# Conditioning loads in their own ring, a first stage on three engines, and a pre-repeated condition vector

## The chip, the cores and the metric

One core of one Trainium2 chip runs the kernel. The metric is the device time of one execution in microseconds (us), lower is better. The kernel before took 1848.71 us (median of 3 runs, 1846.3 to 1849.69).

## The reference

Two decoder layers over 512 tokens with 1024 channels, all in float32. Each layer modulates its input by scale and shift vectors computed from a condition vector `c`, runs a token mixer with three branches, normalises, modulates again and runs a convolutional feed-forward network. Cut to what the change touches:

```python
cond = jax.nn.silu(c)                                   # (1, 1024)
for l in range(2):
    mod = cond @ w_ada[l] + b_ada[l]                    # 6 vectors of 1024
    sh1, sc1, g1, sh2, sc2, g2 = split(mod, 6)
    h = x * (1.0 + sc1) + sh1
    y = _token_mixer(h, ...)                            # retention, HGRN2, convolution, gates, w_out
    x = _layer_norm(ALPHA * x + g1 * y, ln1_g[l], ln1_b[l])
    h = x * (1.0 + sc2) + sh2
    y = _conv_ffn(h, ...)
    x = _layer_norm(ALPHA * x + g2 * y, ln2_g[l], ln2_b[l])
```

## The kernel before

Channels lie on the 128 partitions and tokens along the free axis, so a 1024-channel tensor is 8 tiles of 128 x 512. To keep float32 accuracy every large product is made of three matmuls on rounded parts: an operand is split into a high part `hi` (ScalarE copy to a rounded type) and a rest `lo` (VectorE subtract), and `mm3` adds hi x hi, hi x lo and lo x hi in PSUM (lines 249 to 251).

**Weights** come in chunks of 128 x 1024 (512 KB), in one fixed order per layer. `prefetch` (line 203) takes a tile `wr` of the ring with the tag `raw` (4 buffers), issues its load on SyncE's queue (L215), and writes `wh` (ScalarE, L216) and `wl` (VectorE, L217) into rings of 4. One chunk feeds 24 matmuls. `chunk` calls `prefetch` so that two chunks beyond the one in use have been asked for.

**Conditioning columns.** `ada_col(l, i)` (line 189) makes one column of 128 modulation values: it takes a tile `ar` of the same ring `raw`, loads 512 KB of `w_ada` (L191), multiplies it with `cond` and sums along the row in one VectorE instruction (L195), and adds the bias into `modt` (L196). There are 48 columns for each layer. It is a generator in two steps: the load, then the arithmetic. `cond` is a 128 x 1024 tile that holds silu(c) in every partition.

**The first stage** (lines 692 to 706) does this for j = 0 to 7: two columns of layer 0 (shift and scale of channel tile j), the load of `X[j]`, one weight chunk, and then `hi` (ScalarE, L702), a full-precision copy `f` (GpSimd, L703), `lo = f - hi` (VectorE, L704) and `X[j] *= ALPHA` (GpSimd, L705). Beside it `proj_octo` (line 265) runs 8 passes of 24 matmuls, pass j on the chunk and the `hi`, `lo` of tile j.

**Background work.** `fill` is a list of generators that `tick` advances between groups of 12 matmuls: convolution taps, then `conv_norm` (which makes the branch output `u_c`), then `rest(aux)`, the 24 columns 16 to 39 of the layer. `heads` are the retention and HGRN2 heads. Columns 40 to 47, and the first 16 of layer 1, are put in `fill` during the feed-forward network.

**The branch loop** (lines 760 to 788) takes the branches in the order 1, 0, 2. For each of 4 column pairs jp it runs two gate projections (sigmoid on ScalarE, L767, which frees the PSUM tile) and the branch projection; VectorE multiplies the two (L782), GpSimd adds the product to `ys[j]` (L786), and in the third branch `split` makes `hi` and `lo` of `ys[j]` (L229, L231). The output projection (line 794) then reads all 8 `ys`.

**Order.** The framework lays out each engine's instructions ahead of time, in a fixed order that follows a model of when operands are ready, with the order of the program as priority. On the chip each engine then works through its list in that order. A tile waits until the buffer of its ring that it takes is released.

Of the kernel before, what the change touches and what calls it, by code (L numbers as in the profile page):

```python
# [10 lines left out]
F32 = mybir.dt.float32  # L11
# [3 lines left out]
AF = mybir.ActivationFunctionType  # L15
ALU = mybir.AluOpType
# [4 lines left out]
P = 128  # L21
# [5 lines left out]
FT = DFF // P  # L27
ALPHA = (2.0 * L) ** 0.25
EPS = 1e-5
NB = 47  # L30
NHL = 4
LA = 2
NRAW = 4
TK = 1.7
AUX = 99
TG = 1.1
# [53 lines left out]
def trunk(ctx, tc, xT, cT, pos, ada, bada, wts, cols, lbl, rope_c, decay, hmask, outT):  # L90
    nc = tc.nc
    mm = nc.tensor.matmul
    act = nc.scalar.activation
# [4 lines left out]
    pts = nc.gpsimd.tensor_scalar  # L98

    const = ctx.enter_context(tc.tile_pool(name="const", bufs=1))  # L100
    wp = ctx.enter_context(tc.tile_pool(name="wp", bufs=1))
# [5 lines left out]
    def nm(s):  # L107
        n_[0] += 1
        return f"{s}{n_[0]}"

    def big(dt=F32, w=S):
        return bp.tile([P, w], dt, tag="B", name=nm("b"), bufs=NB)

    def hbuf():
        return bp.tile([P, S], F32R, tag="H", name=nm("h"), bufs=16)
# [4 lines left out]
    def pm():  # L120
        return pp.tile([P, S], F32, tag="pm", name=nm("pm"), bufs=4)
# [8 lines left out]
    def const_tile(shape, name, dt=F32):  # L130
        return const.tile(shape, dt, tag=name, name=name)
# [7 lines left out]
    nc.vector.tensor_copy(avg_r, avg_x)  # L139

    cond = const_tile([P, D], "cond")
    nc.sync.dma_start(cond, cT.partition_broadcast(P))
    act(cond, cond, AF.Silu)
    bad = const_tile([P, 48 * L], "bad")
    nc.sync.dma_start(bad, bada)
# [11 lines left out]
    def mod(l, s, j):  # L157
        return modt[l][:, s * 8 + j:s * 8 + j + 1]
# [28 lines left out]


    def ada_col(l, i):
        raw = wp.tile([P, 1024], F32, tag="raw", name=nm("ar"), bufs=NRAW)  # L190
        nc.sync.dma_start(raw, ada[l, i])  # L191
        o = ADA[i]
        dst = modt[l][:, o:o + 1]
        yield 0.0
        stt(raw, raw, 1.0, cond, ALU.mult, ALU.mult, accum_out=dst)  # L195
        ts(dst, dst, bad[:, 48 * l + o:48 * l + o + 1], 1.0 if o // 8 in (1, 4) else 0.0, ALU.add, ALU.add)  # L196
        yield 1.3
# [5 lines left out]
    def prefetch(n=1):  # L203
        for _ in range(n):
            if wnext[0] == L * NW:
                return
            l, i = divmod(wnext[0], NW)
            wnext[0] += 1
            raw = wp.tile([P, 1024], F32, tag="raw", name=nm("wr"), bufs=NRAW)
            hi = wp.tile([P, 1024], F32R, tag="hi", name=nm("wh"), bufs=NHL)  # L210
            lo = wp.tile([P, 1024], F32R, tag="lo", name=nm("wl"), bufs=NHL)
            n = 512 if l == 0 and i == 0 else 1024
            for o in range(0, 1024, n):
                s = slice(o, o + n)
                nc.sync.dma_start(raw[:, s], wts[l, i][:, s])  # L215
                act(hi[:, s], raw[:, s], AF.Copy)  # L216
                tt(lo[:, s], raw[:, s], hi.bitcast(F32)[:, s], ALU.subtract)  # L217
            ready.append((W_PLAN[l][i][0], (hi, lo)))

    def chunk(kind, ahead=LA):  # L220
        prefetch(ahead + 1 - len(ready))
        k, w = ready.pop(0)
        assert k == kind, (k, kind)
        return w
# [30 lines left out]

    def proj(w, xs, us=TK):
        q = pm()
        n = len(xs)
        for k in range(n):
            mm3(q, sl2(w, 128 * k), xs[k], k == 0, k == n - 1)  # L260
            if k % 4 == 3:
                tick(us)
        return q
# [292 lines left out]
    X = [const_tile([P, S], f"x{j}") for j in range(8)]  # L556
# [136 lines left out]
    for j in range(8):  # L693
        cs = [ada_col(0, 2 * j), ada_col(0, 2 * j + 1)]
        for g in cs:
            next(g)
        nc.sync.dma_start(X[j], xT[j])
        for g in cs:
            next(g)
        prefetch()  # L700
        hi, lo, f = hbuf(), hbuf(), big()
        act(hi, X[j], AF.Identity, bias=mod(0, 0, j), scale=mod(0, 1, j))  # L702
        pts(f, X[j], mod(0, 1, j), mod(0, 0, j), ALU.mult, ALU.add)  # L703
        tt(lo, f, hi.bitcast(F32), ALU.subtract)  # L704
        pts(X[j], X[j], ALPHA, None, ALU.mult)  # L705
        hs.append((hi, lo))

    for l in range(L):
# [3 lines left out]
        acc, u_a, u_b, u_c = [], [None] * NH, [None] * NH, []  # L712
        CS = [big(), big()]
        aux = [ada_col(l, i) for i in range(16, 40)]
        if l == 0:
            tables()
# [43 lines left out]
        for bi, b in enumerate(ORDER):  # L760
            us = (u_a, u_b, u_c)[b]
            for jp in range(4):
                sg = []
                for t in range(2):
                    q = proj(chunk("in"), hs, TG if bi == 2 else TK)
                    s = big()
# [9 lines left out]
                for t in range(2):  # L776
                    j = 2 * jp + t
# [39 lines left out]
        for _ in first:  # L817
            pass

        fill.extend(ada_col(l, i) for i in range(40, 48))  # L820
        gs = []

# [161 lines left out]
```

## Time and profile before

| | before |
|---|---|
| median of 3 runs | 1848.71 us |
| profiled execution, device time | 1850.63 us |
| span of the profile | 1848.5 us |
| granted clock over the span | 0.995 |
| TensorE (PE) busy | 1805.8 us |
| VectorE (DVE) busy | 1292.6 us |
| ScalarE (ACT) busy | 748.4 us |
| GpSimd (POOL) busy | 225.8 us |

The profiled execution took 1850.63 us, 2.1 us more than its span, and 1.9 us more than the median of the runs. All durations below are from this execution. Ends of matmuls are modelled and overlap, so that the spacing of matmul starts, and not their durations, tells the pace.

### The profile page before, as it was taken

The numbers are of one execution on the slowest core, as the hardware profiler recorded it, in microseconds if no ns is written. First come the engines' busy times: TensorE is split into PE (matmuls) and PEld (weight loads), VectorE is DVE, ScalarE is ACT, GpSimd is POOL, SyncE is SP. The second block draws the span as 40 slices with busy tenths as digits, with TensorE's granted clock in tenths as the row PEclk, the third lists the DMA queues.
The fourth block names the chain that finished last, engine by engine and source line by source line (L and its number), as shares of the span: only waits on it lengthen the run. The fifth ranks groups of instructions, "written<-read, shape, count | busy, mean of one in ns | idle before, by whom it ended". The sixth has DMA issues, their size and how long they took to land.

```text
span 1848.5 us, 23499 instructions
## 1 busy us (share of the span) xinstructions
PE 1805.8 (98%) x9156; PEld 1520.1 (82%) x9156; DVE 1292.6 (70%) x2026; ACT 748.4 (40%) x1034; POOL 225.8 (12%) x193
## 2 busy tenths in 40 slices
PE   7999999999999999999999999999999999999997
PEld 5888877888788888888889987778788988888886
DVE  6995565977869756667499565993775896666354
ACT  2434344333337444422263344453523464444222
POOL 3111231042100000000000221320322000000002
PEclk9999999999989999999999999999999999999998
DMA  8512222226614422255222121222474243222221
GB/s 301 197 69 80 75 75 80 91 104 212 230 70 142 144 102 92 102 182 184 93 87 103 69 75 69 80 74 99 161 241 148 92 146 128 103 92 102 92 80 46
DMA packets 63614, 217.81 MB, mean 118 GB/s; under 512 B 7440, under 2 KB 9872, under 8 KB 63504
## 3 DMA queue, kind: packets, MB, share of 16 engines
q1 hardware_dynamic: 63504, 216.32, 34.0%
q8 instruction: 72, 1.18, 0.3%
q14 instruction: 38, 0.31, 0.0%
HBM read 214.19 MB, written 2.10 MB: 117 GB/s over the span
## 4 chain that ended last, share of the span: by engine, by line
PE 81%; DVE 10%; DMA 3%; issue 2%; POOL 2%; ACT 2%; POOLq 0%; SPq 0%; DVEq 0%; ACTq 0%
PE pm L249 24%; PE pm L251 24%; PE pm L250 24%; DMA ar<-ada 3%; DVE wl L217 2%; PE ps L477 2%; POOL b L786 1%; DVE ar L195 1%; DVE b L383 1%; DVE x L642 1%; PE po L552 1%; PE ps L544 1%; DVE b L782 1%; PE ps L250 1%; PE ps L251 0%
## 5 line engine op out<-in xcount | busy, mean ns | idle before, releaser
L249 PE MATMUL pm<-h,wh 128*128 128x512 f32 (+1 forms) x1568 | 612.7, 391 | 13.7 <-ACT wh L216 12.1
L251 PE MATMUL pm<-h,wl 128*128 128x512 f32 (+1 forms) x1568 | 602.6, 384 | 0.1
L250 PE MATMUL pm<-h,wh 128*128 128x512 f32 (+1 forms) x1568 | 601.6, 384 | 0.0
L217 DVE TENSOR_TENSOR wl<-wr,wh 128x1024 fp32r<-128x1024 f32 (+1 forms) x301 | 376.4, 1253 | 250.5 <-ACT wh L216 249.4
L216 ACT ACTIVATE wh<-wr 128x1024 fp32r<-128x1024 f32 (+1 forms) x301 | 317.1, 1055 | 489.3 <-PE pm L250 387.2
L249 PEld LDWEIGHTS pm<-h,wh 128*128 128x128 f32 x1568 | 295.5, 188 | 72.9 <-ACT wh L216 12.1
L251 PEld LDWEIGHTS pm<-h,wl 128*128 128x128 f32 x1568 | 295.0, 188 | 61.1 <-DVE wl L217 3.1
L250 PEld LDWEIGHTS pm<-h,wh 128*128 128x128 f32 x1568 | 295.4, 188 | 58.7 <-issue 1.9
L249 PE MATMUL pm<-b,wh 128*128 128x512 f32 (+1 forms) x764 | 280.6, 367 | 5.6 <-ACT b L229 4.2
L250 PE MATMUL pm<-b,wh 128*128 128x512 f32 (+1 forms) x764 | 279.6, 366 | 0.3 <-DVE b L231 0.2
L251 PE MATMUL pm<-b,wl 128*128 128x512 f32 (+1 forms) x764 | 279.0, 365 | 0.0
L383 DVE SCALAR_TENSOR_TENSOR b<-b,cols,b 128x511 f32<-128x511 f32 (+14 forms) x240 | 171.6, 769 | 0.0
L249 PEld LDWEIGHTS pm<-b,wh 128*128 128x128 f32 x764 | 144.8, 190 | 30.3 <-ACT b L229 5.4
L250 PEld LDWEIGHTS pm<-b,wh 128*128 128x128 f32 x764 | 144.9, 190 | 24.5 <-DVE b L231 1.5
L251 PEld LDWEIGHTS pm<-b,wl 128*128 128x128 f32 x764 | 145.0, 190 | 22.8
L195 DVE SCALAR_TENSOR_TENSOR ar<-ar,cond 128x1024 f32<-128x1024 f32 x96 | 123.8, 1296 | 57.1 <-DMA ar<-ada 56.9
L229 ACT ACTIVATE b<-b 128x512 fp32r<-128x512 f32 x88 | 55.5, 630 | 232.8 <-DVE b L832 109.2
L231 DVE TENSOR_TENSOR b<-b,b 128x512 fp32r<-128x512 f32 x88 | 61.1, 694 | 53.8 <-ACT b L229 53.6
L490 POOL TENSOR_TENSOR b<-b,b 128x256 f32<-128x256 f32 x64 | 56.4, 881 | 324.1 <-PE ps L477 217.3
L786 POOL TENSOR_TENSOR b<-b,b 128x512 f32<-128x512 f32 x32 | 57.2, 1786 | 234.9 <-DVE b L782 222.5
L249 PE MATMUL pm<-wh,h 128*128 128x256 f32 x256 | 73.6, 288 | 0.0
L250 PE MATMUL pm<-wl,h 128*128 128x256 f32 x256 | 72.3, 283 | 0.6 <-DVE wl L217 0.6
(205 smaller groups left out, 1904.1 us busy)
## 6 DMA issues: line engine op xcount, KB each, us to landing
wr<-wts SPq DMA_DIRECT2D x299, 512.0 KB, 3.5
ar<-ada SPq DMA_DIRECT2D x96, 512.0 KB, 4.3
x<-xT SPq DMA_DIRECT2D x8, 256.0 KB, 5.9
b<-decay SPq DMA_DIRECT2D x8, 256.0 KB, 3.7
outT<-b SPq DMA_DIRECT2D x16, 128.0 KB, 1.8
b<-hmask SPq DMA_DIRECT2D x3, 256.0 KB, 5.9
cond<-cT SPq DMA_DIRECT2D x1, 512.0 KB, 4.5
wr<-wts SPq DMA_DIRECT2D x2, 256.0 KB, 7.3
```

Source lines behind the costliest of these rows:

```text
L195: stt(raw, raw, 1.0, cond, ALU.mult, ALU.mult, accum_out=dst)
L216: act(hi[:, s], raw[:, s], AF.Copy)
L217: tt(lo[:, s], raw[:, s], hi.bitcast(F32)[:, s], ALU.subtract)
L229: act(hi, src, AF.Copy)
L231: tt(lo, src, hi.bitcast(F32), ALU.subtract)
L249: mm(dst, a[0], b[0], start=first, stop=False)
L250: mm(dst, a[0], b[1], start=False, stop=False)
L251: last[0] = mm(dst, a[1], b[0], start=False, stop=end)
L383: stt(a[:, d:S], us[i][:, 0:S - d], col(l, "cw", 4 * (CK - 1 - d) + i0 + i), a[:, d:S], ALU.mult, ALU.add)
L477: mm(z[:, 64 * i:64 * (i + 1)], ke[:, sl], rhs, start=True, stop=True)
L490: ptt(kv[:, :, 0, :], kv[:, :, 0, :], fv[:, :, 1:2].broadcast_to([P, nb, m]), ALU.mult)
L786: ptt(ys[j], ys[j], sg[t], ALU.add)
```

## The change

- `cT`, the input that `cond` is loaded from, becomes a 128 x 1024 array with the same row repeated by the host; the load reads 128 rows in place of one row 128 times.
- `ada_col` takes its tile from a ring of its own, tag `ada`, 3 buffers. `raw` keeps 4 buffers, now for weights alone.
- In the first stage GpSimd's two instructions go to ScalarE: `f` becomes a second `act` like `hi`, `X[j] *= ALPHA` an `act` with AF.Copy.
- The ring `B` of 128 x 512 tiles has 48 buffers in place of 47.
- The scratch area for software-made DMA descriptors is 1024 bytes; with it there is space for the new buffers.

```diff
-NB = 47
+NB = 48
+NADA = 3
@@
     cond = const_tile([P, D], "cond")
-    nc.sync.dma_start(cond, cT.partition_broadcast(P))
+    nc.sync.dma_start(cond, cT)
@@ def ada_col(l, i):
-        raw = wp.tile([P, 1024], F32, tag="raw", name=nm("ar"), bufs=NRAW)
+        raw = wp.tile([P, 1024], F32, tag="ada", name=nm("ar"), bufs=NADA)
@@
         act(hi, X[j], AF.Identity, bias=mod(0, 0, j), scale=mod(0, 1, j))
-        pts(f, X[j], mod(0, 1, j), mod(0, 0, j), ALU.mult, ALU.add)
+        act(f, X[j], AF.Identity, bias=mod(0, 0, j), scale=mod(0, 1, j))
         tt(lo, f, hi.bitcast(F32), ALU.subtract)
-        pts(X[j], X[j], ALPHA, None, ALU.mult)
+        act(X[j], X[j], AF.Copy, scale=ALPHA)
@@
-        "cT": np.ascontiguousarray(a["c"][0]),
+        "cT": np.repeat(a["c"], 128, axis=0),
@@
-    nc = _bacc.Bacc("TRN2", target_bir_lowering=False, num_devices=1)
+    nc = _bacc.Bacc("TRN2", target_bir_lowering=False, num_devices=1, dynamic_dma_scratch_size=1024)
```

## Rows read from the trace of the kernel before

**Rows 1.** The page, part 1: busy time of each engine, share, instructions.
```profile
PE 1805.8 (98%) x9156; PEld 1520.1 (82%) x9156; DVE 1292.6 (70%) x2026; ACT 748.4 (40%) x1034; POOL 225.8 (12%) x193
```

**Rows 2.** Timeline of the start: start, duration, engine, line, operation [idle before <-releaser].
```profile
4.82 4.55 SPq L191 DMA_DIRECT2D ar<-ada  x2
...
7.78 1.23 DVE L195 SCALAR_TENSOR_TENSOR ar<-ar,cond 128x1024 f32<-128x1024 f32 x1 [6.58 <-DMA ar<-ada]
...
9.41 0.43 SPq L697 DMA_DIRECT2D x<-xT  x1
...
12.07 0.79 PE L249 MATMUL pm<-h,wh 128*128 128x512 f32 x1 [12.07 <-ACT wh L216]
```

**Rows 3.** The page, part 6: DMA issues, count, KB each, median us to landing.
```profile
wr<-wts SPq DMA_DIRECT2D x299, 512.0 KB, 3.5
...
cond<-cT SPq DMA_DIRECT2D x1, 512.0 KB, 4.5
```

**Rows 4.** Timeline of PE: second pass of the first stage begins; next projection begins.
```profile
19.81 0.39 PE L249 MATMUL pm<-h,wh 128*128 128x512 f32 x1
...
59.53 0.40 PE L249 MATMUL pm<-wh,h 128*128 128x256 f32 x2
60.55 0.39 PE L250 MATMUL pm<-wl,h 128*128 128x256 f32 x1 [0.62 <-DVE wl L217]
```

**Rows 5.** Window: busy us (instructions) of each engine, granted clock, DMA share, GB/s.
```profile
1500.00:1550.00 50.00, 50.00 (x222) 41.44 (x221) 41.35 (x62) 23.95 (x32) 0.00 (x0) 1.00 0.49 166
```

**Rows 6.** Groups by line, 12 to 53 us: count, busy us, mean ns, idle before.
```profile
L702 ACT ACTIVATE h<-x,mod 128x512 fp32r<-128x512 f32 x7 | 5.7, 817 | 28.3 <-DVE mod L196 28.3
...
L704 DVE TENSOR_TENSOR h<-b,h 128x512 fp32r<-128x512 f32 x8 | 5.5, 693 | 7.6 <-POOL b L703 7.6
```

**Rows 7.** Timeline of PE, layer 0: last branch projection, output projection, marker L582.
```profile
494.19 0.39 PE L249 MATMUL pm<-b,wh 128*128 128x512 f32 x1
...
501.16 0.50 PE L249 MATMUL pm<-b,wh 128*128 128x512 f32 x1 [1.34 <-ACT b L767]
507.46 0.56 PE L249 MATMUL pm<-b,wh 128*128 128x512 f32 x1 [1.94 <-ACT b L229]
...
511.70 0.80 PE L249 MATMUL pm<-b,wh 128*128 128x512 f32 x1 [2.29 <-ACT b L229]
...
526.48 0.40 PE L582 MATMUL ps<-b,avg_r 128*128 128x512 f32 x1
```

**Rows 8.** Timeline of PE, layer 1: the same two ends.
```profile
1413.33 0.39 PE L249 MATMUL pm<-b,wh 128*128 128x512 f32 x1
...
1435.55 0.40 PE L582 MATMUL ps<-b,avg_r 128*128 128x512 f32 x1
```

**Rows 9.** Window in layer 0's stretch: columns as in the window above.
```profile
508.00:518.00 10.00, 7.54 (x17) 5.20 (x17) 4.45 (x6) 2.05 (x3) 2.11 (x1) 0.50 0.32 114
```

**Rows 10.** Timeline of DVE: late gate product, last conditioning column of layers 0 and 1.
```profile
492.61 0.69 DVE L782 TENSOR_TENSOR b<-pm,b 128x512 f32<-128x512 f32 x1
...
500.75 1.21 DVE L195 SCALAR_TENSOR_TENSOR ar<-ar,cond 128x1024 f32<-128x1024 f32 x1
...
1389.86 1.23 DVE L195 SCALAR_TENSOR_TENSOR ar<-ar,cond 128x1024 f32<-128x1024 f32 x1 [0.55 <-DMA ar<-ada]
```

**Rows 11.** Waits: DVE from 403 to 502 us; SyncE's queue from 390 to 500 us.
```profile
DVE ar L195 <- DMA ar<-ada: 15.7, 11, 4.3
...
SPq L191 <- DVE wl L217: 18.1, 6, 6.2
```

**Rows 12.** Timeline: end of `u_c` on DVE, and the first PE instruction that reads it.
```profile
435.79 0.68 DVE L231 TENSOR_TENSOR b<-b,b 128x512 fp32r<-128x512 f32 x1
...
444.31 0.39 PE L249 MATMUL pm<-b,wh 128*128 128x512 f32 x1
```

**Rows 13.** Timeline of SyncE's queue: conditioning loads among weight loads, layer 0.
```profile
403.25 0.33 SPq L191 DMA_DIRECT2D ar<-ada  x1
...
409.15 5.98 SPq L191 DMA_DIRECT2D ar<-ada  x2
```

## The prediction, made before the changed kernel had run

> **What bounds the kernel now.** I read the page first: TensorE is busy 1805.8 of 1848.5 us [rows 1], so outside it there are 42.7 us, and 12.07 of these pass before the first matmul [rows 2]. An edit to loads, VectorE, ScalarE or GpSimd can therefore win only where TensorE waits or runs at its lower clock. I then took windows of 50 us over the whole span to find where that is. Three places matter: the start, the first stage (to 60 us), and one stretch at 500 to 520 us, the only one in the middle of the kernel where the granted clock falls. Everywhere else a window looks like the one in [rows 5]: 222 matmuls in 50 us, 0.225 us each.
>
> The third place is the largest, and it has a twin. From the first matmul of the last branch projection to the marker matmul L582, layer 0 takes 526.48 - 494.19 = 32.3 us [rows 7]; layer 1 does the same work in 1435.55 - 1413.33 = 22.2 us [rows 8]. The 10.1 us between them are idle time of 1.3 + 1.9 + 2.3 us [rows 7] and about 10 us at a granted clock of 0.50, the 1.2 GHz level, in which 17 matmuls started and not 44 [rows 9]. What is late there is VectorE's list: the gate product L782 runs at 492.61 [rows 10]; TensorE had left its operands before it began the two gate projections that end at 494.19, 48 matmuls or 10.8 us earlier, at about 483.4 [rows 5, 7]. It is 9 us late, and GpSimd's add and ScalarE's split wait for it. VectorE is late because it is still doing conditioning columns, the last at 500.75, after the last branch matmul has been issued. In layer 1 the last one is at 1389.86, 23 us before the last branch projection even begins [rows 10, 8]. From 403 to 502 us VectorE stood still 15.7 us for loads of these columns; SyncE's queue in turn stood 18.1 us with a column's load that needed a buffer which a weight chunk held [rows 11].
>
> **The change, part by part.**
>
> *The start.* The load of `cond` lands 4.5 us after its issue with nothing ahead of it in the queue; a weight chunk of the same size lands in 3.5 [rows 3]. If the repeated read is what costs the difference, the loads behind it come 1.0 us sooner, the first column among them, for which VectorE waits until 7.78 [rows 2]. If it is not, the gain is 0. Nothing in the trace excludes that 128 separate rows are read more slowly than one, so I let it lose as much. I take the middle of the gain, **-0.5 us** (+1.0 to -1.0), since a plain load of this size is the nearest row to the new one. The Trainium skill (DMA: Bandwidth & Descriptors, Why small descriptors are slow) says that each packet carries a fixed cost, so that small ones move slowly; by that the time lost ahead of the first column belongs to the bias table, loaded in 128 rows of 384 bytes between the two, which stays; the start would gain nothing, and the total would be 0.5 us higher.
>
> *The first stage.* Seven passes take 59.53 - 19.81 = 39.7 us, 5.67 each [rows 4]; 24 matmuls at 0.225 are 5.4 us [rows 5]. VectorE sets the pace, and of its waits one counts: it stands 7.6/8 = 0.95 us a pass until GpSimd's `f` is there [rows 6]. With `f` on ScalarE behind `hi`, that wait would grow: two passes of 0.82 us [rows 6] in a row, 1.65 us. But VectorE then need not wait. The weight load of a pass no longer needs a buffer that a column holds, and the next pass's first column is in flight one conversion earlier, since the third `ada` buffer is released by a column and not by `wl`; either gives VectorE 1.2 us of work to put there. Nothing reads `X[j]*ALPHA` before the output projection, after 501 us [rows 7]; on ScalarE it costs about 0.8 us of some 4.0 idle a pass (28.3 over seven in [rows 6]). What is late next is TensorE itself, at 5.4 us. So the pace can gain 7 x 0.27 = 1.9 us; it could lose 8 x 0.7 = 5.6 us if the wait stays unfilled. I take **-1.3 us**, near the filled end, because the load that would fill it has its buffer. The 0.62 us that the next projection waits for its weights [rows 4] follows from the same lateness: **-0.5 us** (0 to -0.6).
>
> *The ring of the columns.* SyncE issues in written order: the load of the second `X` tile needs no buffer, and still went at 9.41, behind the columns that were stuck from 4.82 [rows 2]. So a column's load cannot pass the weight loads in front of it; what changes is what each waits for. Before, each of the four buffers went round weights and columns alike, and column 17 was issued at 409.15, 6 us after column 16, and 18 in the 6 us after that [rows 13]. With three buffers of their own, 16, 17 and 18 go back to back at about 398 to 403, and the next weight load needs only a weight buffer. The columns start 5 us earlier, and most of the 15.7 us that VectorE stood for them [rows 11] goes. Together that moves the last column from 502 to about 482 to 490 us; it needs to move by 9, the lateness of L782. Then layer 0's stretch should cost what layer 1's does. The saving lies between 0 (nothing moves) and 10.1 us; I take **-9.0 us**, nearest to the twin, since layer 1 shows this very code with earlier columns. A column's load that waits for its own ring still blocks the weight loads behind it on SyncE; these now have up to four chunks of 5.4 us loaded ahead, so I price that at nothing, and at one 5.4 us chunk if a column waits longer than that.
>
> *The rest costs nothing.* No TensorE wait in the trace ends on a `B` buffer, and no queue for software-made DMAs appears on the page, so `NB` and the scratch size have nothing to buy; the 48th buffer may shift the laid-out order, 1 us either way.
>
> Sum: -0.5 - 1.3 - 0.5 - 9.0 = **-11.3 us**. The profiled execution took 1850.6, so 1839.3 on its scale; it lay 1.9 us above the median of the runs, so I forecast a median of **1837.4 us**.
>
> **The rivals.**
> 1. *The columns end no earlier.* SyncE's written order is the limit: each column's load still stands behind a weight load that waits for a conversion, VectorE's list is laid out for loads that land sooner than they do, and the 15.7 us return. For it: the written order [rows 2]. Against it: the 18.1 us that columns waited for weight conversions [rows 11]. Only the first stage gains: 1848.7 - 2.3 = 1846.4 us. This is also the case in which the separate buffers don't do what they say.
> 2. *Half a cure.* The columns end some 5 us earlier; one stall is left and the clock still falls once. Half of 10.1 stays: 1848.7 - 2.3 - 5 = 1841.4 us.
> 3. *Slower: the columns run into `u_c`.* Columns that start earlier fall among the convolution norm's steps on VectorE. `u_c` is ready at 436.5 us and TensorE reads it at 444.31 [rows 12], 7.8 us of slack, while a column takes 1.2 us and its bias 0.2. From six columns more in front of `u_c`, TensorE idles there and the clock falls, a cost for which the only price in the trace is 10.1 us [rows 7, 8]. Against it: VectorE's waits for loads in that stretch are long enough to take most of those columns. If layer 0's saving fails as well: 1848.7 - 2.3 + 10.1 = 1856.5 us.
>
> **How the numbers follow.** Forecast 0.58, rival 2 0.12, rival 1 0.18, rival 3 0.12. About 0.2% (3.7 us) can be told from no change: faster is below 1845.0, which holds the forecast, rival 2 and a little of rival 1: 0.72. Rival 1's rest is the same, 0.16; rival 3 is slower, 0.12. The low end of the range takes every bound of the gain (1.0 + 1.9 + 0.6 + 10.1 = 13.6, 1835.1) and 3 us for the shifted order and the spread of the runs: 1832. The high end takes in rival 1 and 2 us of that spread: 1848.5. Rival 3 and parts of the others, under 2 in 10, are left out.
>
> **What would show it.** The start: the first matmul before 12.07, at 11.6. The first stage: L704 no longer has 7.6 us of waits in front of it and the passes come every 5.4 to 5.5 us; if they come every 6 or more, ScalarE's chain has taken the place of GpSimd's. The ring: column loads three in a row near 400 us, VectorE's waits for `ar` in 400 to 500 us well below 15.7, the last layer 0 column before 490, no granted clock below 1.00 near 510, and 22 to 23 us from the last branch projection to L582. The prediction is wrong if the last column is still near 500, or if a clock drop appears at another place, most likely where the third branch first reads `u_c`.

## The result: slower, by 13 us

The changed kernel takes 1861.9 us (median of 6 runs, 1861.3 to 1864.8) against 1849.1 for the kernel before (6 runs, 1846.3 to 1851.3): a ratio of 1.007, 95% interval 1.006 to 1.008. The forecast was 1837.4 us. The profiled execution has a span of 1860.2 us, 11.7 more than before.

The page of the changed kernel, part 1, answers to [rows 1]. All lines of the code are one higher than before:

```profile
PE 1807.5 (97%) x9156; PEld 1522.5 (82%) x9156; DVE 1292.1 (69%) x2026; ACT 759.5 (41%) x1050; POOL 207.9 (11%) x177
```

TensorE and VectorE do the same work for the same time. What changed is when VectorE does it. Its column products alone (L196; columns: VectorE's busy time and instruction count, clock, DMA share, GB/s; each column has two records):

```profile
60.00:160.00 100.00, 7.71 (x12) 1.00 0.37 127
160.00:310.00 150.00, 58.22 (x90) 0.99 0.67 229
310.00:400.00 90.00, 17.01 (x26) 1.00 0.50 168
400.00:453.00 53.00, 25.16 (x32) 0.90 0.59 199
453.00:1850.00 1397.00, 0.00 (x0) 1.00 0.26 89
```

All 80 columns after the first stage, layer 1's 48 among them, are done by 453 us. Before, layer 0's last was at 500.75 and layer 1 made its own far later [rows 10]. They now lie among the heads of layer 0 (in this kernel until 322.6 us) and its convolution norm. Windows of the whole core there (PE, PEld, DVE, ACT, POOL busy; clock; DMA), and of the stretch in which the clock fell before:

```profile
150.00:200.00 50.00, 46.91 (x264) 39.13 (x263) 46.49 (x92) 20.13 (x31) 12.51 (x11) 1.00 0.65 221
200.00:250.00 50.00, 46.72 (x236) 37.45 (x236) 45.12 (x97) 20.14 (x31) 8.34 (x8) 0.97 0.76 256
250.00:300.00 50.00, 45.61 (x228) 35.01 (x227) 49.17 (x85) 21.04 (x35) 16.68 (x14) 1.00 0.59 201
400.00:450.00 50.00, 42.10 (x172) 33.91 (x172) 48.66 (x70) 16.75 (x23) 25.35 (x13) 0.90 0.63 211
500.00:550.00 50.00, 49.84 (x220) 40.93 (x219) 26.04 (x34) 17.75 (x23) 6.83 (x4) 1.00 0.27 93
```

VectorE is busy for 45 to 49 us of each 50 in the first four, and there TensorE stands still for 3 to 8 us of each 50. In the last, where [rows 7, 9] showed idle time and a clock of 0.50, TensorE is now full at full clock: the gain that the prediction looked for is there. Its two ends, in answer to [rows 7], are 22.2 us apart, as in the twin [rows 8]:

```profile
518.00 0.39 PE L250 MATMUL pm<-b,wh 128*128 128x512 f32 x1
...
540.22 0.40 PE L583 MATMUL ps<-b,avg_r 128*128 128x512 f32 x1
```

How a column holds up TensorE, in the heads: it has eleven waits of over 0.25 us there, 11.3 us in all, where before it had one of 0.5 us. First the longest of them, then VectorE's list ahead of it (timelines of PE and DVE; in brackets the idle time before, and what ended it):

```profile
233.05 0.56 PE L244 MATMUL po<-b,avg_r 128*128 128x512 f32 x1 [2.79 <-DVE mod L197]
```
```profile
227.38 1.23 DVE L196 SCALAR_TENSOR_TENSOR ar<-ar,cond 128x1024 f32<-128x1024 f32 x1 [2.53 <-DMA ar<-ada]
...
231.01 1.21 DVE L196 SCALAR_TENSOR_TENSOR ar<-ar,cond 128x1024 f32<-128x1024 f32 x1
232.16 0.08 DVE L196 DVE_READ_ACCUMULATOR ar<-ar,cond 128x1 f32 x1
232.16 0.74 DVE L431 SCALAR_TENSOR_TENSOR b<-po,cols,b 128x512 f32<-128x512 f32 x1
232.82 0.20 DVE L197 TENSOR_SCALAR mod<-mod,bad 128x1 f32<-128x1 f32 x1
```

L244 reads no column. It writes a `po` tile (in PSUM), and L431 is the VectorE instruction that empties one; it ends at 232.9 and TensorE starts at 233.05. The view names L197, the next instruction on VectorE, which ends at 233.0; as L244 has nothing of L197, I take it for L431. Two columns stand in front of L431, with the conversion of a weight chunk between them (in the lines left out), and the first column had VectorE idle for 2.5 us until its load landed. VectorE works its list in order, so everything behind a column waits for the column's load too. The second place is the convolution norm, where L409 must end before ScalarE can square, GpSimd add the squares and TensorE sum them (timelines of DVE, POOL, PE):

```profile
422.53 1.30 DVE L196 SCALAR_TENSOR_TENSOR ar<-ar,cond 128x1024 f32<-128x1024 f32 x1 [0.94 <-DMA ar<-ada]
423.82 1.23 DVE L196 SCALAR_TENSOR_TENSOR ar<-ar,cond 128x1024 f32<-128x1024 f32 x1
424.97 2.48 DVE L409 SCALAR_TENSOR_TENSOR b<-po,b 128x512 f32<-128x512 f32 x4
...
430.73 2.27 DVE L196 SCALAR_TENSOR_TENSOR ar<-ar,cond 128x1024 f32<-128x1024 f32 x1
```
```profile
429.68 2.24 POOL L398 TENSOR_TENSOR b<-b,b 128x512 f32<-128x512 f32 x1
431.99 2.12 POOL L399 TENSOR_TENSOR b<-b,b 128x512 f32<-128x512 f32 x1
```
```profile
416.39 0.39 PE L246 MATMUL po<-b,avg_r 128*128 128x512 f32 x1
...
434.83 0.79 PE L244 MATMUL po<-b,avg_r 128*128 128x512 f32 x1 [7.14 <-ACT b L237]
...
436.97 0.63 PE L250 MATMUL pm<-b,wh 128*128 128x512 f32 x1
438.25 0.63 PE L250 MATMUL pm<-b,wh 128*128 128x512 f32 x1
```

Six columns lie between 405.7 and 420, two more stand right in front of L409. TensorE had the mean that L409 reads at 416.8, and L409 starts at 424.97, 8.2 us later; in between VectorE makes three columns. In strided_columns (below), where a column is short, the same instruction follows its mean within 0.1 us. TensorE stands 7.1 us, and after it the same matmuls start 1.28 us apart where 0.68 was the pace: the granted clock is 0.50, the 1.2 GHz level, from 436 to 441.

### The profile page after: what moved, and what is told of

Its sections match the earlier page's. It is cut to its first block, busy times and chain, and to the rows that moved or that the text cites. A ratio compares the mean times of both kernels' runs of the same rounds, so it can differ in the third digit from the quotient of the medians.

```text
span 1860.2 us, 23501 instructions
## 1 busy us (share of the span) xinstructions
PE 1807.5 (97%) x9156; PEld 1522.5 (82%) x9156; DVE 1292.1 (69%) x2026; ACT 759.5 (41%) x1050; POOL 207.9 (11%) x177
## 4 chain that ended last, share of the span: by engine, by line
PE 77%; DVE 14%; issue 3%; DMA 2%; POOL 2%; ACT 1%; SPq 0%; POOLq 0%; DVEq 0%; ACTq 0%
PE pm L250 24%; PE pm L251 24%; PE pm L252 23%; DVE ar L196 3%; DVE wl L218 3%; DVE b L384 2%; DMA ar<-ada 2%; PE ps L478 2%; POOL b L787 1%; DVE x L643 1%; DVE b L783 1%; DVE b L490 1%; PE ps L251 1%; ACT h L665 1%; PE ps L252 1%
## 5 line engine op out<-in xcount | busy, mean ns | idle before, releaser
L196 DVE SCALAR_TENSOR_TENSOR ar<-ar,cond 128x1024 f32<-128x1024 f32 x96 | 127.1, 1339 | 19.2 <-DMA ar<-ada 19.1
L250 PE MATMUL pm<-wh,h 128*128 128x256 f32 x256 | 73.9, 289 | 0.0
L252 PE MATMUL pm<-wh,h 128*128 128x256 f32 x256 | 72.5, 283 | 0.0
```

Of the source, the lines that this page charges most:

```text
L250: mm(dst, a[0], b[0], start=first, stop=False)
L252: last[0] = mm(dst, a[1], b[0], start=False, stop=end)
```

## The experiments

Each kernel was run beside the kernel before. To compare places, the spans between TensorE's own marks are read from each trace: A, start to the first matmul of the second token projection (121.54 before); B, from there to the first matmul on a branch output (309.53), the heads; C, to the last branch projection of layer 0 (494.19), which holds the convolution norm; D, to the marker L582 (526.48); E, to the last pair of matmuls. In us, as the difference to the kernel before, whose spans are 121.5, 188.0, 184.7, 32.3 and 1309.3:

```
                     A      B      C      D      E     sum   median  ratio [95% interval]
after              -1.8  +14.8  +10.8  -10.1   -2.0   +11.7  1861.9  1.007  [1.006, 1.008]
ring_alone         -0.8  +13.0   +8.9  -10.1   -2.1    +8.9  1860.1  1.0058 [1.0043, 1.0073]
no_ring            -0.1    0.0   -0.2   -0.2   -0.4    -0.9  1849.3  0.9996 [0.9986, 1.0005]
loads_in_order     -2.5    0.0   -0.3  -10.1   +0.9   -11.9  1839.0  0.9943 [0.9928, 0.9957]
strided_columns    -2.1   +9.2   +0.3  -10.1   -2.0    -4.7  1845.5  0.9979 [0.9970, 0.9989]
dummy_traffic      -1.4    0.0   -0.2  -10.1   +1.4   -10.3  1839.7  0.9941 [0.9926, 0.9956]
small_columns      -1.2   +3.7   -0.9  -10.1   -2.1   -10.6  1838.3  0.9933 [0.9916, 0.9949]
next_layer_early   -1.9    0.0    0.0  -10.1   -3.3   -15.3  1834.5  0.9917 [0.9903, 0.9932]
order_gpsimd_stage -0.5    0.0   -0.2  -10.1   -0.6   -11.3  1839.9  0.9947 [0.9932, 0.9962]
```

How many weight chunks stand ahead of the columns on SyncE's laid-out list explains the rows (columns 16 to 39 and 40 to 47 of layer 0, then all of layer 1):

```
before, no_ring        65 to 78, 91 to 103; 131 to 147, 211 to 223, 241 to 253
loads_in_order         the same, but for a shift by one near 217
after, ring_alone      all 80 between 16 and 68
strided_columns        all 80 between 16 and 52
```

**The ring alone.** The kernel before, plus the ring and the smaller scratch area:

```diff
+NADA = 3
...
-        raw = wp.tile([P, 1024], F32, tag="raw", name=nm("ar"), bufs=NRAW)
+        raw = wp.tile([P, 1024], F32, tag="ada", name=nm("ar"), bufs=NADA)
```

> The kernel before with one part of the change alone: the columns' own ring of three buffers (with the smaller scratch area that makes room for it). 47 `B` buffers, the first stage with GpSimd and the condition read as one row stay as before. Theory A (the own ring lets the columns' loads be laid out up to 1000 us earlier than they are written, and their VectorE instructions then stand in front of the heads and the convolution norm of layer 0): nearly all of the loss is here; without the 1.75 us that the first stage gave by the second token projection, 1862 to 1865 us, the first branch projection near 325 us. Theory B (the moved loads hold up SyncE's queue or the weights' transfers): the same time, so this run does not part A from B. Theory C (the first stage, the 48th buffer or the condition is at fault and the ring does what was predicted of it): about 1849 - 10 = 1839 us.

Measured 1860.1 us, 2 us under the range of theories A and B; the heads lose 13.0 us and the stretch with the norm 8.9, in the same places as in the changed kernel and 2 us less in each. Theory C falls: the ring makes the loss.

**The change without the ring.** The changed kernel with that one line undone.

> The changed kernel with the columns' tiles back in the weights' ring; the condition repeated, the first stage without GpSimd and the 48th buffer stay. Theories A and B: the loads of the columns stand where they stood in the kernel before, the layer 0 loss of 24.7 us is gone and so is the gain of 10 us in the transition to the output projection; what the first stage gives remains, 1849.0 - 1.75 = 1847.3 us. Theory C: 1860 us or more.

Measured 1849.3 us, no difference from before (within 0.14%). Loss and gain both go, as theories A and B say, but the 1.75 us of the first stage go as well; only 0.1 is left by the second token projection. With GpSimd out and the old ring, the first token projection starts at 60.33, later than the 59.53 of [rows 4].

**Column loads in written order.** The changed kernel; `lastw` is the weight load traced last:

```diff
-        nc.sync.dma_start(raw, ada[l, i])
+        if lastw[0] is None:
+            nc.sync.dma_start(raw, ada[l, i])
+        else:
+            with tc.issue_after(lastw[0].ins):
+                nc.sync.dma_start(raw, ada[l, i])
```

> The changed kernel with one thing added: a column's load is kept behind the latest weight load that stands before it in the program, so that SyncE's list has the written order that the prediction took for granted. The ring of three, the first stage and the condition stay as changed. Theories A and B: the columns are made in 400 to 500 us again, the stalls between 153 and 441 us are gone, and the gains of the first stage (1.75 us) and of the transition (10.1 us) stay: 1849.0 - 1.75 - 10.1 = 1837.2 us. Theory C: 1860 us. If the prediction's picture of the ring was wrong as well as its premise, the transition's 10 us come back: 1847 us.

Measured 1839.0 us, 10.4 less than the 1849.4 of the kernel before on that chip, and 23 less than the changed kernel, which differs by that rule alone. B and C are back at the old spans while D keeps its 10.1 us. This was the prediction's premise, put into the code, and with it come the signs that the prediction named for the ring: layer 0's last column starts at 480.01 in place of 500.75 [rows 10], VectorE's waits for column loads from 403 to 502 us fall from 15.7 [rows 11] to 3.2 us, and the granted clock is 1.00 from 500 to 515.

```profile
480.01 1.23 DVE L202 SCALAR_TENSOR_TENSOR ar<-ar,cond 128x1024 f32<-128x1024 f32 x1 [0.21 <-DMA ar<-ada]
```
```profile
DVE ar L202 <- DMA ar<-ada: 3.2, 5, 1.2
```

The windows that lost above (PE, PEld, DVE, ACT, POOL; clock; DMA):

```profile
150.00:200.00 50.00, 50.00 (x297) 42.55 (x297) 32.49 (x49) 22.01 (x34) 12.09 (x13) 1.00 0.24 82
200.00:250.00 50.00, 49.59 (x264) 40.08 (x263) 27.66 (x44) 23.52 (x36) 13.50 (x14) 1.00 0.19 67
250.00:300.00 50.00, 49.52 (x225) 38.99 (x224) 28.57 (x43) 23.37 (x37) 10.95 (x10) 1.00 0.24 85
400.00:450.00 50.00, 49.61 (x219) 40.76 (x218) 46.51 (x77) 23.48 (x31) 14.62 (x9) 1.00 0.66 239
```

Moving the loads moved both VectorE's work and the DMA traffic (0.59 to 0.76 of the DMA engines in the heads against 0.2), so this run doesn't part theory A from theory B. The next three do.

**Early loads, short arithmetic.** The changed kernel; the first stage keeps the whole product:

```diff
-        stt(raw, raw, 1.0, cond, ALU.mult, ALU.mult, accum_out=dst)
+        n = 1 if i < 16 and l == 0 else 8
+        stt(raw[:, ::n], raw[:, ::n], 1.0, cond[:, ::n], ALU.mult, ALU.mult, accum_out=dst)
```

> The changed kernel, but the 80 columns after the first stage multiply and sum only every eighth element of their 1024 (part of the computation is left out): the loads keep their size, their ring and their early places, and each VectorE instruction is cut from 1.23 us to some 0.2 us. Theory A (VectorE's time in front of the heads): the stalls between 153 and 441 us go, while the gains stay: 1836 to 1840 us. Theory B (SyncE's queue or the transfers): the loads still come early, so the loss stays: 1858 to 1863 us.

Measured 1845.5 us, between the two. In C the loss is gone (+0.3 against +10.8): there it was the columns' arithmetic. In the heads 9.2 of 14.8 us stay. Waits in 143 to 317 us (engine, line, tile, waited for; total us, times, longest), with line numbers one higher than in the changed kernel:

```profile
DVE ar L197 <- DMA ar<-ada: 29.3, 22, 3.2
...
PE ps L546 <- DVE b L548: 2.6, 1, 2.6
```

VectorE, done sooner with each column, now stands at the next one until its load lands, and what is behind it waits for that instead. In the changed kernel these waits were 7.0 us. So the two are not terms to be added: arithmetic and waiting fill the same gap. That TensorE's longest wait here, the 2.6 us for L548, comes of them is argued and not shown: VectorE stood for a load last at 285 us, and was busy from there until L548 ended at 299.3. And the loads are also as early, and the DMA engines busier (0.70 to 0.86), than in the changed kernel, so theory B still had 9 us to stand on.

**Loads that nobody waits for.** loads_in_order, and for 27 weight chunks:

```diff
+            if l == 0 and 27 <= i < 54:
+                for _ in range(3):
+                    d = wp.tile([P, 1024], F32, tag="ada", name=nm("dd"), bufs=NADA)
+                    nc.sync.dma_start(d, ada[1, i % 48])
```

> loads_in_order plus 81 loads of 512 KB into the columns' ring that nothing reads (this is added work). They are laid out as early as the changed kernel's columns were: between the 16th and the 42nd weight load, in runs of up to ten on SyncE's queue. The real columns stay in their written places, so VectorE has nothing of these loads. In strided_columns 9.1 us were still lost between 143 and 317 us, with the loads early and their arithmetic short. Theory A1 (that rest is VectorE standing at a column whose load has not landed, 29.3 us in 22 waits there): loads that no instruction waits for cost nothing, 1839 us, first branch projection at 307 us. Theory B (SyncE's queue or the transfers hold up the weights): 9 us come back, 1846 to 1850 us, first branch projection at 314 us or later.

Measured 1839.7 us, as without the added loads, and B differs by 0.0. From 143 to 317 us SyncE's queue stood 44.0 us for them (61.1 in the whole run), and until the last of them at 242 us the DMA engines were busier than in the changed kernel:

```profile
SPq L228 <- DMA dd<-ada: 44.0, 27, 4.5
```
```profile
150.00:200.00 50.00, 50.00 (x287) 42.78 (x286) 32.27 (x48) 21.79 (x33) 11.96 (x12) 1.00 0.85 305
200.00:250.00 50.00, 49.59 (x274) 39.79 (x275) 26.81 (x42) 22.81 (x34) 12.76 (x13) 1.00 0.84 303
```

TensorE is full at 305 GB/s. Theory B falls for the heads, and strided_columns had cleared C with the loads early; a column costs through VectorE's list, not through its bytes.

**Small loads, small arithmetic, early places.** The changed kernel; the columns after the first stage load and sum 128 elements.

> The changed kernel, but the 80 columns after the first stage load and sum only 128 of their 1024 elements (part of the computation is left out): early places on SyncE and VectorE as in the changed kernel, an eighth of the bytes, some 0.2 us of arithmetic, and short waits. Theories A and B: both the time and the waits are gone, so the loss between 153 and 441 us goes: 1837 to 1840 us. If the early places alone cost something (more instructions in front of the heads, whatever they last), some 3 to 5 us stay: 1842 us.

Measured 1838.3 us. C is free again and 3.7 of the 14.8 us stay in the heads, with 18.6 us of VectorE's waits for the small loads. So the total came out as theories A and B expected and the place as the last sentence did: an instruction that costs 0.28 us still makes VectorE's list wait for its load.

**A better place.** loads_in_order, with layer 1's columns written into layer 0's feed-forward network:

```diff
-        aux = [ada_col(l, i) for i in range(16, 40)]
+        aux = [ada_col(0, i) for i in range(16, 40)] if l == 0 else []
...
-        fill.extend(ada_col(l, i) for i in range(40, 48))
+        if l == 0:
+            fill.extend(ada_col(0, i) for i in range(40, 48))
+            fill.extend(ada_col(1, i) for i in range(12))
...
-            fill.extend(ada_col(1, i) for i in range(16))
+            fill.extend(ada_col(1, i) for i in range(12, 48))
...
-TD = 1.0
+TD = 2.2
```

> loads_in_order with layer 1's columns written elsewhere: all 48 in layer 0's feed-forward network (12 in the up projections, 36 in the down projections, whose credit for background work goes from 1.0 to 2.2 us) and none in layer 1. In loads_in_order 5.4 us are lost in layer 1 between 1282 and 1303 us, where TensorE waits 1.7 us for the convolution norm and its clock falls, while the columns 16 to 39 of layer 1 are made. VectorE is busy only 30 of 50 us in layer 0's feed-forward network. Theory A (VectorE's list decides; columns cost nothing where it has room): 2 to 5 us less than loads_in_order, 1834 to 1837 us. If the loss there is the norm's own chain and not the columns: 1839 us.

Measured 1834.5 us: 14.7 less than the kernel before on that chip and, each against the kernel before on its own chip, some 4 less than loads_in_order. In loads_in_order the same norm stalls in layer 1 in the same manner (PE, then GpSimd's adds and VectorE's columns):

```profile
1297.74 0.49 PE L250 MATMUL po<-b,avg_r 128*128 128x512 f32 x1 [1.68 <-ACT b L243]
```
```profile
1291.19 2.26 POOL L403 TENSOR_TENSOR b<-b,b 128x512 f32<-128x512 f32 x1
1293.41 2.27 POOL L404 TENSOR_TENSOR b<-b,b 128x512 f32<-128x512 f32 x1
1295.76 1.26 POOL L405 TENSOR_TENSOR b<-b,b 128x512 f32<-128x512 f32 x1
```
```profile
1290.12 2.19 DVE L202 SCALAR_TENSOR_TENSOR ar<-ar,cond 128x1024 f32<-128x1024 f32 x1
1292.24 2.30 DVE L202 SCALAR_TENSOR_TENSOR ar<-ar,cond 128x1024 f32<-128x1024 f32 x1
```

The kernel before waited 0.5 us at this sum, at a granted clock of 1.00 from 1290 to 1320 us, so that even in written order the earlier columns cost something here, in the way that rival 3 described. With the columns gone TensorE has no wait between 1280 and 1305 us, where its window was 22.45 of 25 us at a clock of 0.93:

```profile
1280.00:1305.00 25.00, 25.00 (x112) 20.64 (x111) 11.57 (x13) 10.61 (x14) 10.69 (x8) 1.00 0.30 106
```

The columns cost nothing where they went, though 590 to 960 us now hold 63 us of VectorE's time for them: TensorE is full there, 50.00 of 50 us at 1.00 from 700 to 750 and from 850 to 900. In the table, E is at -2.0 or below in each kernel that makes no columns in layer 1's branches and above it in the others; but three kernels with one and the same layer 1 (loads_in_order, dummy_traffic, order_gpsimd_stage) differ by 1.9 us there, so that this is a sign and no measure.

**Written order, GpSimd in the first stage.** loads_in_order with `f` and `X[j] *= ALPHA` back on GpSimd.

> loads_in_order with the first stage's two instructions on GpSimd again: own ring, written order, condition repeated. It prices the part of the change that takes GpSimd out. The first stage's end (second pass to first token projection) should come 0.7 to 1.5 us later than in loads_in_order: 1840 to 1840.5 us. If the own ring alone feeds VectorE there, no difference: 1839 us.

Measured 1839.9 us against 1839.0, less than the intervals part. By the marks, A is 2.0 us longer and E 1.5 shorter. Of the 2.0, 0.9 lie after the first token projection's start: it takes 62.0 us in the three kernels with GpSimd in the first stage (before, ring_alone, this one) and 61.1 in the others, no_ring among them. Those 0.9 us are the only firm price here: the first token projection does begin 1.1 us later than in loads_in_order, as expected, but among the six kernels with the ring and the same first stage its start ranges over 1.3 us too (57.96 to 59.22).

## Why the prediction was wrong

**What bounds the kernel, and the twin: right.** The stretch from the last branch projection to L582 went from 32.3 to 22.2 us in every kernel with the ring. The term was put at -9.0 between 0 and -10.1; it measured -10.1. In the changed kernel it came because layer 0's columns were long done, and not as the prediction had it; in loads_in_order it came as predicted, by a last column that starts at 480.01.

**The step that failed** is the sentence "SyncE issues in written order [...] So a column's load cannot pass the weight loads in front of it". It was read from the second `X` load, which needed no buffer and still went behind stuck columns [rows 2]. That row shows that SyncE works its list in order; it says nothing of how the list was laid out. In the kernel before, columns and weights took turns in one ring, and a tile can only take the buffer that the one before it in the ring has left, so the ring held the columns in written order. The change took that away. With three buffers of their own the columns depend on nothing but each other, and the list was laid out with 80 of them between the 16th and 68th weight chunk, where before they stood between the 65th and 253rd. What they then cost VectorE's list, 14.8 us in the heads and 10.8 with the norm, stands nowhere in the sum. That no_ring has the old places and ring_alone the new ones shows that it is the ring; loads_in_order, at 1839.0 against the forecast 1837.4, shows that the sum stood on this one sentence.

**Rival 3 had the mechanism and one of the two places; its total is near by luck.** It put the extra columns in front of `u_c`'s steps, as the 7.1 us wait inside the convolution norm shows, and priced one stall with its clock drop at 10.1 us, taken from another stall; C measured +10.8. It thought of some six columns moved by a few us within 400 to 502 us, and not of 45 columns (90 records in the table above) between 160 and 310 us, where the heads lost another 14.8. And its total, 1856.5, joined the price to a saving that fails, while the saving came: the 10.1 us that it left out and the 14.8 that it did not foresee partly cancel. The prediction's last line of what would show it wrong, a clock drop "most likely where the third branch first reads `u_c`", points to the right chain one step late.

**The first stage.** L705 no longer waits for another engine's `f`, as predicted of [rows 6], but VectorE's waits were moved and not filled: from 12 to 53 us it stands 4.2 us for column loads and 4.8 for ScalarE's `wh`, 9.0 in all, where it stood 8.9 before, 7.6 of them for `f`. They no longer come in every pass, though, and the conversion of a weight chunk takes VectorE 1.22 us on average where it took 1.33 beside GpSimd. How much of the gain comes of which wasn't tried.

The seven passes take 38.07 us (20.59 to 58.66) in place of 39.7, 5.44 each as forecast: -1.65 where -1.3 was put. The next projection, 61.1 us in place of 62.0 and without the wait of 0.62, gave -0.9 where -0.5 was put. Against this the first pass takes 8.5 us in place of 7.7, a loss of 0.8 that the sum left out. Start and first stage together were put at -2.3 us (-0.5, -1.3, -0.5); by the second token projection the changed kernel had -1.8, and the six kernels with this first stage and the ring (after, loads_in_order, strided_columns, dummy_traffic, small_columns, next_layer_early) lie between -1.2 and -2.5. The warning that ScalarE's longer chain loses what VectorE doesn't fill fits no_ring: without the ring the stage takes 48.2 us from first matmul to first token projection, 0.7 more than before and the longest of all kernels here; the six take 46.3 to 47.4.

**The load of the condition.** It landed 3.4 us after its issue in place of 4.5 [rows 3], and ScalarE began on it at 4.17 in place of 5.22; in all ten kernels it takes 4.5 or 4.6 us read as one row and 3.3 to 3.5 read as 128. In the changed kernel the first column still started at 7.77, for its own load, and the first matmul at 12.06 in place of 12.07:

```profile
4.17 1.06 ACT L144 ACTIVATE cond<-cond 128x1024 f32<-128x1024 f32 x1 [2.16 <-DMA cond<-cT]
...
7.77 1.22 DVE L196 SCALAR_TENSOR_TENSOR ar<-ar,cond 128x1024 f32<-128x1024 f32 x1 [6.58 <-DMA ar<-ada]
```

The Trainium skill (DMA: Bandwidth & Descriptors, Why small descriptors are slow) had been cited for the other end, a start that gains nothing because the small packets of the bias table stay ahead of the first column. The two traces agree with that end, 0.0, but they can't settle a term of 0.5 us: the other kernels that read the repeated condition begin their first column between 7.34 and 8.18 us, and ring_alone, which reads it as before, at 7.24. No run took the bias table away, so that it is the reason isn't shown either.

**"I price that at nothing"**, of a column's load that blocks the weight loads behind it on SyncE: dummy_traffic, with 44.0 us of such waits from 143 to 317 us and no loss in the heads, shows this right there.

**The rest.** The 48th `B` buffer and the scratch size showed nothing: no_ring carries the 48th and is within 0.2 us of before in C and D.

## What to carry to other kernels

A shared buffer ring is also an ordering constraint: before taking a stream of loads out of it, ask what will hold them in place, and say it in the code if nothing does. An early load is cheap, but its consumer moves with it into an in-order list, and whatever stands behind it then waits for the load and the arithmetic; so look at where the consuming engine has room (here layer 0's feed-forward network), not at the share it is busy on average. When a saving arrives and the time still rises, cut the run into spans between fixed marks on the bounding engine and compare them one by one.

## What the runs showed of the hardware

A VectorE product of two 128x1024 operands takes 1.22 us, and 2.05 to 2.30 us when GpSimd adds two tensors beside it; GpSimd's 128x512 add takes 1.3 us alone and 2.1 to 2.3 us then, as the rows at 429 to 434 and 1290 to 1297 us show. Both are long there because each starts while the other is running; of a pair that stands alone only the one that starts second is stretched. In strided_columns an add from 409.13 us took 1.29 us and VectorE's weight conversion beside it, from 409.16, 2.34; in the kernel before the conversion from 407.90 took 1.22 and the add from 407.91 took 2.37. The columns thus lengthened the norm's chain on GpSimd too. The Trainium skill (GPSIMD Engine Reference, Specifications) says that GpSimd shares its SBUF interface with VectorE and that the two contend when a VectorE instruction has two SBUF inputs; these rows agree. How much of the norm's 10.8 us is this and how much the order of the list was not tried.

Summing every eighth of 1024 elements took 0.42 us (median of 80), summing 128 elements that lie side by side 0.28: with the same number of elements, the step of eight cost half as much again.
